# A two-block sequence model on one core: the second block's input scaled once, its products read from PSUM, and all low parts of the recurrent mixer on VectorE

## The chip, the cores and the metric

The kernel runs on one core of a Trainium2 chip, as one launch. The metric is the time of the whole program on the device, in microseconds (us). TensorE is the matrix engine (PE in the profile), VectorE is DVE, ScalarE is ACT, GpSimd is POOL, and SyncE (SP) issues most of the DMA transfers.

## The reference

Two residual blocks over 256 tokens with 2048 features, all in float32. The first block (a state-space mixer beside latent attention, and a feed-forward part) is not touched by the change. The second block computes, cut to what matters:

```
u = rms_norm(h, norm1_g);  P = u @ w_in_2
z, xbc, dt_raw = parts of P                      # state-space mixer
pr = rest of P;  pr = pr + (prev_token(pr) - pr) * mu   # recurrent mixer
xbc = silu(causal_conv4(xbc));  xs, B, C = xbc
y_ssd = group_norm(scan(xs, dt, A, B, C) + D * xs, times silu(z)) * g
r, k, v, wd, ad, gd = pr                         # three of 2048, and low-rank inputs
y_rwkv = per head: S = S*decay + (S a) b^T + v k^T;  y = S r, then norm, bonus, gate
h = h + concat(y_ssd, y_rwkv) @ w_out_2
h = h + (silu(v @ w_gate) * (v @ w_up)) @ w_down,  v = rms_norm(h, norm2_g)
out = rms_norm(h, norm_f_g)
```

The input h of the second block is the first block's final norm of its own sum. Both norms are one factor per token and a gain per feature, so that P = R(token) * ((gains * sum) @ w_in_2).

## The kernel before

Features lie on the 128 partitions and the 256 tokens along the free dimension, so a matrix product makes an output tile of 128 features by 256 tokens in one PSUM bank. Each f32 operand is split into a rounded high part and a low part (the difference), and a product is the sum of high x low, high x high and low x high. `split` makes the two parts of an input tile (ScalarE the high, VectorE the low one). `piece` loads 512 KB of weights (`raw`), ScalarE rounds them (`wh`, L329) and VectorE or GpSimd subtracts (`wl`, L335): `self.pl` is the share of pieces whose subtraction goes to GpSimd. It is 0 in the state-space stage, 1 in the recurrent stage and on into the output product, and 0.25 in the feed-forward part. `gemm` runs 2 pieces and 16 x 3 matmuls of 256 columns in these stages (`self.one`), and after each 16th part calls `tick`, which steps the background work of the recurrent mixer.

The stages of the second block, with their times in the profile: `block2_pre` (norm factors, from 1206 us), `ssd_phase` (4 products for low-rank inputs and step sizes with `ssd_dt`, 8 for B and C, 16 pairs for x and z; to about 1506), `rwkv_phase` (16 times k, v and r, then the first half of the output product with the state-space result; to about 2190), `block2_out` (second half of the output product) and `ffn2`.

Here the products are made on the unscaled input tiles (`xx`), and the norm's factor R is multiplied into every product when it leaves PSUM: `shift_mix` and `conv_silu` call `evac` (L381, VectorE, PSUM times R into a tile `ev`), then a ScalarE step and one or three VectorE steps (L1113, the token shift; L1128, the convolution's taps) read `ev`. `ssd_pair` does the same for z with Rh = R / 2 (tile `zh`). Two PSUM banks (`acc`) take turns for the products.

In the recurrent stage the order of TensorE's instructions is the program's, written by hand with `tick` counts (`TK`); the other engines' orders, and all of the state-space stage, come from a scheduler that simulates the engines. Heads are worked in 8 groups of two tiles. For each group there are masked products (L1446 to L1464), an inverse of a triangular block by a loop of 30 small VectorE steps (L1494, L1496) with round trips through DRAM, and then 4 recurrence steps: TensorE, the copy `ws` (L1569), TensorE, the copies into `UV` (L1574), TensorE, the new state (L1583).

Of the kernel before, what the change touches and what calls it, by code (L numbers as in the profile page):

```python
# [10 lines left out]
F32 = mybir.dt.float32  # L11
# [7 lines left out]
P = 128  # L19
T = 256  # L20
# [203 lines left out]
class K:  # L224
# [851 lines left out]
    def block2_pre(self, p1):  # L1076
# [14 lines left out]
        self.bcast(r2, self.R)  # L1091
        nc.gpsimd.tensor_scalar(self.Rh, self.R, 0.5, None, ALU.mult)
        self.bcast(r1, self.R1)
# [12 lines left out]

    def shift_mix(self, p, out, i):

        nc = self.nc
        a = self.t(tag="ev")  # L1110
        self.evac(p, a, self.R, eng=nc.gpsimd)
        nc.scalar.activation(out, a, AF.Copy, scale=self.omm[:, i:i + 1])
        nc.vector.scalar_tensor_tensor(out[:, 1:], a[:, :T - 1], self.v("mu", i), out[:, 1:], ALU.mult, ALU.add)  # L1113

    def conv_silu(self, p, out, i):

        nc = self.nc
        a = self.t(tag="ev")
        self.evac(p, a, self.R, eng=nc.gpsimd)
# [57 lines left out]
    def ssd_group(self, g, pb, pc):  # L1177

        nc = self.nc
        B = self.t(tag="sB", bufs=2)  # L1180
        self.conv_silu(pb, B, 16 + g)
        C = self.CC[:, g]
        self.conv_silu(pc, C, 20 + g)
        p = self.ps(384, "pcs")
        nc.tensor.transpose(p[:, :P], B[:, :P], self.ident)
        for b in range(2):
            sl = slice(b * P, b * P + P)
            nc.tensor.matmul(p[:, P + b * P:2 * P + b * P], B[:, sl], C[:, sl], start=True, stop=True)
        nc.scalar.activation(self.BT[:, g], p[:, :P], AF.Copy)
        nc.vector.tensor_tensor(self.CC[:, 4 + g].rearrange("p (c t) -> p c t", c=2),  # L1190
                                p[:, P:].rearrange("p (c t) -> p c t", c=2),
                                self.tri.unsqueeze(1).to_broadcast([P, 2, P]), op=ALU.mult)

    def ssd_pair(self, j, px, pz):
# [67 lines left out]
    def ssd_phase(self, xx):  # L1262
        nc, A = self.nc, self.A
        W = A["w_in2"]
        self.tri = self.sd.tile([P, P], F32, name="tri")
        nc.scalar.dma_start(self.tri, A["cst3"])
        self.CC = self.b([8, T], "hh0")
        self.BT = self.b([4, P], "hh1")
        p = self.gemm(W[0], 16, xx)
        x0 = self.t(tag="ev")  # L1270
        self.shift_mix(p, x0, 48)
        self.twd = self.m2.tile([P, T], F32, name="twd")
        nc.scalar.activation(self.twd, x0, AF.Tanh)
        self.ssd_dt(x0)
        self.tad = self.m2.tile([P, T], F32, name="tad")
        self.shift_mix(self.gemm(W[1], 16, xx), self.tad, 49)
        self.tgd = self.m2.tile([P, 2, T], F32, name="tgd")
        for i in range(2):
            x0 = self.t(tag="ev")
            self.shift_mix(self.gemm(W[2 + i], 16, xx), x0, 50 + i)  # L1280
            nc.scalar.activation(x0, x0, AF.Tanh, scale=0.5)
            nc.vector.tensor_scalar(self.tgd[:, i], x0, 1.0, 0.5, ALU.add, ALU.mult)
        for g in range(4):
            pb = self.gemm(W[4 + g], 16, xx)
            pc = self.gemm(W[8 + g], 16, xx)
            self.ssd_group(g, pb, pc)
        for j in range(16):
            px = self.gemm(W[12 + j], 16, xx)
            pz = self.gemm(W[28 + j], 16, xx)
            for _ in self.ssd_pair(j, px, pz):  # L1290
                pass


    def rwkv_alloc(self):
        nc, c = self.nc, self.rw
        xb = self.b([16, T], "X")
        bk = xb[:, 0:8].rearrange("p (s c) t -> p s (c t)", s=4).rearrange("p s (c t) -> p s c t", c=4)
        nc.gpsimd.memset(bk, 0.0)
# [4 lines left out]

        self.BK = xb[:, 8:16].rearrange("p (i h) t -> p i h t", i=4).rearrange("p i h (c n) -> p i h c n", c=4)
# [4 lines left out]
        self.Gs = self.b([4, 2, 4, 64], "B0")  # L1309
        self.UV = self.b([4, 2, 4, 64], "B1")  # L1310
        nc.gpsimd.memset(self.L, 0.0)
# [305 lines left out]
    def rwkv_phase(self, xx):  # L1617
        nc, V = self.nc, self.nc.vector
        W = self.A["w_in2"]
        self.rwkv_alloc()  # L1620
        self.pl = 1
        self.rs_ = {}
        with self.tc.manual_schedule(engines={mybir.EngineType.PE}):
# [16 lines left out]

            xs = self.xx_new()
            for k in range(16):
# [32 lines left out]
    def block2(self, xx, p1, upto=99):  # L1675
# [3 lines left out]
        with ExitStack() as es0:  # L1679
            self.m2 = es0.enter_context(self.tc.tile_pool(name="m2", bufs=1))  # L1680
            with ExitStack() as es:
# [3 lines left out]
                self.sd = self.ph = es.enter_context(self.tc.tile_pool(name="sd", bufs=1))  # L1685
                self.ssd_phase(xx)
            if upto < 4:
# [24 lines left out]
    def block2_out(self):  # L1712
        nc, A = self.nc, self.A
        V = nc.vector
        x0 = self.b([8, 2, T], "X", F32R)
        x1 = [self.b([4, 2, T], f"xx{i}", F32R) for i in range(2)]

        def xs(k):
            return x0[:, k] if k < 8 else x1[k // 4 - 2][:, k % 4]

        for k in range(16):
# [3 lines left out]
        for i in range(2):  # L1725
            nc.sync.dma_start(self.hh[i], self.hd2[:, 8 * i:8 * i + 8])
        self.x2 = [self.b([4, 2, T], t, F32R) for t in ("B0", "B1", "xx2", "xx3")]
        pf = Sums(self, 16)
        for n in range(16):
            p = self.gemm(A["w_out2"][16 + n], 16, xs)  # L1730
            self.add_h(p, n)
            self.split(self.x2[n // 4][:, n % 4], self.h(n), self.v("norm2_g", n))
            pf.add(self.h(n))
        self.pf = pf.out

    def ffn2(self):
# [5 lines left out]

        def x2(k):
            return self.x2[k // 4][:, k % 4]

        for half in range(2):
            a0 = self.b([8, 2, T], "X", F32R)
            a1 = [self.b([4, 2, T], f"xx{i}", F32R) for i in range(2)]
            a2 = self.f.tile([P, 6, 2, T], F32R, name=self.nm("ac"), tag="ac")

            def ac(k, a0=a0, a1=a1, a2=a2):
                return a0[:, k] if k < 8 else a1[k // 4 - 2][:, k % 4] if k < 16 else a2[:, k - 16]

# [72 lines left out]
```

## Time and profile before

| what | value |
|---|---|
| median of 3 runs | 3052.31 us (3050.88 to 3054.97) |
| the profiled execution's own time | 3044.86 us |
| its span, first to last instruction | 3043.1 us |
| TensorE busy, share of the span | 2826.2 us, 93% |
| VectorE busy | 2004.5 us, 66% |
| ScalarE busy | 1521.5 us, 50% |
| GpSimd busy | 1267.5 us, 42% |
| mean granted TensorE clock | 0.965 |
| low parts on VectorE, on GpSimd | 522 of 1280 ns mean, 351 of 2396 ns mean |

Busy time is the time in which an engine has an instruction under way; matmuls overlap in a pipeline, so a busy TensorE need not be at its peak. The granted clock is a share of 2.4 GHz. A wait is put down to the instruction that ended last before the waiting one began.

### The profile page before, as it was taken

The numbers are of one execution on the slowest core, as the hardware profiler recorded it, in microseconds if no ns is written. First come the engines' busy times: TensorE is split into PE (matmuls) and PEld (weight loads), VectorE is DVE, ScalarE is ACT, GpSimd is POOL, SyncE is SP. The second block draws the span as 40 slices with busy tenths as digits, with TensorE's granted clock in tenths as the row PEclk, the third lists the DMA queues.
The fourth block names the chain that finished last, engine by engine and source line by source line (L and its number), as shares of the span: only waits on it lengthen the run. The fifth ranks groups of instructions, "written<-read, shape, count | busy, mean of one in ns | idle before, by whom it ended". The sixth has DMA issues, their size and how long they took to land.

```text
span 3043.1 us, 54949 instructions
## 1 busy us (share of the span) xinstructions
PE 2826.2 (93%) x21648; PEld 2543.3 (84%) x21648; DVE 2004.5 (66%) x3272; ACT 1521.5 (50%) x2553; POOL 1267.5 (42%) x877
## 2 busy tenths in 40 slices
PE   6766999999999999999979888888899999999998
PEld 6755988888888888999878878778888888888887
DVE  9994578885388866887676777775365554355544
ACT  6527555554455555555445444453354444444454
POOL 6555663333333344011465444444694333233333
PEclk8878999999999999999999999999999999999999
DMA  4222355556655566555443333334655556655565
GB/s 164 84 78 70 110 169 184 186 187 182 189 185 186 189 179 222 186 180 182 149 131 111 109 106 107 108 112 155 215 181 187 189 187 187 192 191 186 189 186 154
DMA packets 178979, 490.38 MB, mean 161 GB/s; under 512 B 44416, under 2 KB 61600, under 8 KB 178208
## 3 DMA queue, kind: packets, MB, share of 16 engines
q1 hardware_dynamic: 176992, 483.13, 50.1%
q8 instruction: 170, 2.79, 0.4%
q0 software_dynamic: 288, 2.10, 0.2%
q10 hardware_dynamic: 1440, 1.63, 0.2%
q14 instruction: 89, 0.73, 0.1%
HBM read 474.17 MB, written 12.62 MB: 160 GB/s over the span
## 4 chain that ended last, share of the span: by engine, by line
PE 69%; DVE 8%; DMA 3%; issue 1%; POOL 1%; ACT 1%; SPq 1%; POOLq 0%; DVEq 0%; ACTq 0%
PE acc L353 34%; PE acc L354 17%; PE acc L349 5%; PE acc L350 4%; PE acc L351 4%; DVE ti L1494 1%; DVE D L1496 1%; POOL wl L335 1%; DVE kvr L1113 1%; ACT wh L329 1%; PE pm L1446 1%; DMA N<-n_d 1%; PE pc L1329 1%; DMA raw<-in_w_in_dram 0%; DVE kvr L1457 0%
## 5 line engine op out<-in xcount | busy, mean ns | idle before, releaser
L329 ACT ACTIVATE wh<-raw 128x1024 fp32r<-128x1024 f32 (+2 forms) x873 | 907.8, 1041 | 948.0 <-PE acc L353 459.2
L335 POOL TENSOR_TENSOR wl<-raw,wh 128x1024 fp32r<-128x1024 f32 (+1 forms) x351 | 839.6, 2396 | 815.0 <-ACT wh L329 785.0
L335 DVE TENSOR_TENSOR wl<-raw,wh 128x1024 fp32r<-128x1024 f32 (+2 forms) x522 | 667.8, 1280 | 481.7 <-ACT wh L329 478.2
L353 PE MATMUL acc<-xx,wh 128*128 128x512 f32 x2496 | 885.8, 395 | 0.0
L354 PE MATMUL acc<-xx,wl 128*128 128x256 f32 x2496 | 704.3, 282 | 0.0
L349 PE MATMUL acc<-xx,wh 128*128 128x256 f32 x1968 | 599.7, 305 | 19.6 <-ACT wh L329 7.4
L351 PE MATMUL acc<-xx,wl 128*128 128x256 f32 x1968 | 567.8, 289 | 15.1 <-POOL wl L335 11.0
L350 PE MATMUL acc<-xx,wh 128*128 128x256 f32 x1968 | 568.0, 289 | 0.0
L353 PEld LDWEIGHTS acc<-xx,wh 128*128 128x128 f32 x2496 | 469.9, 188 | 110.6
L354 PEld LDWEIGHTS acc<-xx,wl 128*128 128x128 f32 x2496 | 468.9, 188 | 4.5 <-POOL wl L335 3.9
L349 PEld LDWEIGHTS acc<-xx,wh 128*128 128x128 f32 x1968 | 386.0, 196 | 33.4 <-ACT wh L329 8.1
L351 PEld LDWEIGHTS acc<-xx,wl 128*128 128x128 f32 x1968 | 385.8, 196 | 18.2 <-POOL wl L335 12.5
L350 PEld LDWEIGHTS acc<-xx,wh 128*128 128x128 f32 x1968 | 387.0, 197 | 2.8 <-issue 1.2
L353 PE MATMUL acc<-B,wh 128*128 128x512 f32 x960 | 341.1, 394 | 0.0
L354 PE MATMUL acc<-B,wl 128*128 128x256 f32 x960 | 269.6, 281 | 2.0 <-DVE wl L335 1.0
L353 PE MATMUL acc<-X,wh 128*128 128x512 f32 x640 | 230.5, 397 | 2.2 <-ACT wh L329 2.2
L390 POOL TENSOR_TENSOR ev<-ev,R 128x256 f32<-128x256 f32 x88 | 70.7, 803 | 353.5 <-PE acc L353 322.2
L353 PEld LDWEIGHTS acc<-B,wh 128*128 128x128 f32 x960 | 180.6, 188 | 41.7
L213 POOL TENSOR_TENSOR qa<-qa,sq 128x256 f32<-128x256 f32 x86 | 88.4, 1028 | 281.7 <-issue 133.7
L354 PEld LDWEIGHTS acc<-B,wl 128*128 128x128 f32 x960 | 179.8, 187 | 3.1 <-POOL wl L335 1.6
L354 PE MATMUL acc<-X,wl 128*128 128x256 f32 x640 | 180.8, 282 | 1.6 <-POOL wl L335 1.6
L353 PEld LDWEIGHTS acc<-X,wh 128*128 128x128 f32 x640 | 121.4, 190 | 29.5 <-ACT wh L329 2.4
(491 smaller groups left out, 4228.9 us busy)
## 6 DMA issues: line engine op xcount, KB each, us to landing
raw<-in_w_up_dram SPq DMA_DIRECT2D x264, 512.0 KB, 3.7
raw<-in_w_in_dram SPq DMA_DIRECT2D x213, 512.0 KB, 3.7
raw<-in_w_down_dram SPq DMA_DIRECT2D x128, 448.0 KB, 3.8
raw<-in_w_out_dram SPq DMA_DIRECT2D x96, 512.0 KB, 3.7
raw<-in_w_gate_dram SPq DMA_DIRECT2D x88, 512.0 KB, 4.2
raw<-in_w_down_dram SPq DMA_DIRECT2D x64, 512.0 KB, 4.2
raw<-in_w_glu_dram SPq DMA_DIRECT2D x8, 512.0 KB, 3.4
cb<-cs_d SPq DMA_DIRECT2D x16, 256.0 KB, 4.1
```

What stands on the lines that cost most here:

```text
L213: nc.gpsimd.tensor_tensor(self.acc, self.acc, sq, op=ALU.add)
L329: nc.scalar.activation(h, r, AF.Copy)
L335: eng.tensor_tensor(l, r, h.bitcast(F32), op=ALU.subtract)
L349: nc.tensor.matmul(p[:, :T], h, x[:, 1], start=first, stop=False)
L350: nc.tensor.matmul(p[:, :T], h, x[:, 0], start=False, stop=False)
L351: nc.tensor.matmul(p[:, :T], l, x[:, 0], start=False, stop=last)
L353: nc.tensor.matmul(p, h, x.rearrange("p a b -> p (a b)"), start=first, stop=False)
L354: nc.tensor.matmul(p[:, T:], l, x[:, 0], start=False, stop=last)
L390: (eng or nc.vector).tensor_tensor(out, s, mul, op=ALU.mult)
L1113: nc.vector.scalar_tensor_tensor(out[:, 1:], a[:, :T - 1], self.v("mu", i), out[:, 1:], ALU.mult, ALU.add)
L1329: self.nc.tensor.matmul(out[hs], lhsT[hs], rhs[hs], start=start, stop=stop)
L1446: nc.tensor.matmul(p[:, P * c:P * c + P], z[:, c], AR[:, c].rearrange("p a t -> p (a t)"), start=True, stop=True)
```

## The change

After the first use of the input, each of the 16 input tiles is made anew from the sum h, with the gains and R multiplied in, and split (`rescale`, four tiles behind each of the first four products, into buffers X, B0, B1). The 4 first products and the 8 for B and C still use the unscaled tiles and `evac`; the 32 of the pairs and the 48 of the recurrent mixer use the scaled ones, and what follows reads PSUM directly (`rms` returns the bank). The factor 1/2 of z goes into the tanh's scale and the last product of a pair, so Rh is not made there. `self.pl = 1` is taken out of the recurrent stage: the share stays 0 until `ffn2` sets 0.25, so all low parts there and in the output product are VectorE's. The buffers of the recurrent mixer move from X, B0, B1 to xx0 to xx3, and those of the output product and the feed-forward part change to fit.

```diff
-        nc.gpsimd.tensor_scalar(self.Rh, self.R, 0.5, None, ALU.mult)
+        self.cg = self.m2.tile([P, 16], F32, name="cg2")
+        nc.vector.tensor_tensor(self.cg, self.vs("final_norm_w"), self.vs("norm1_g"), op=ALU.mult)
...
+    def x16(self):
+        a, b, c = self.b([8, 2, T], "X", F32R), self.b([4, 2, T], "B0", F32R), self.b([4, 2, T], "B1", F32R)
+        return lambda k: a[:, k] if k < 8 else b[:, k - 8] if k < 12 else c[:, k - 12]
+    def rescale(self, xs, ks):
+        for k in ks:
+            t = self.t(tag="ev")
+            self.nc.vector.scalar_tensor_tensor(t, self.h(k), self.cg[:, k:k + 1], self.R, ALU.mult, ALU.mult)
+            self.split(xs(k), t)
+    def rms(self, p, scaled):
+        if scaled:
+            return p[:, :T]
         a = self.t(tag="ev")
-        self.evac(p, a, self.R, eng=nc.gpsimd)
+        self.evac(p, a, self.R)
+        return a
+    def shift_mix(self, p, out, i, scaled=True):
+        a = self.rms(p, scaled)
...
-        self.evac(pz, zh, self.Rh, eng=nc.gpsimd)
-        nc.scalar.activation(th, zh, AF.Tanh)
-        V.scalar_tensor_tensor(zh, th, 1.0, zh, ALU.add, ALU.mult)
+        nc.scalar.activation(th, pz[:, :T], AF.Tanh, scale=0.5)
+        V.scalar_tensor_tensor(zh, th, 1.0, pz[:, :T], ALU.add, ALU.mult)
...
-        V.tensor_tensor(y, x, zh, op=ALU.mult)
+        V.scalar_tensor_tensor(y, x, 0.5, zh, ALU.mult, ALU.mult)
...
-        self.CC = self.b([8, T], "hh0")
-        self.BT = self.b([4, P], "hh1")
         p = self.gemm(W[0], 16, xx)
         x0 = self.t(tag="ev")
-        self.shift_mix(p, x0, 48)
+        xs = self.x16()
+        self.shift_mix(p, x0, 48, False)
+        self.rescale(xs, range(4))
...
-            px = self.gemm(W[12 + j], 16, xx)
-            pz = self.gemm(W[28 + j], 16, xx)
+            px = self.gemm(W[12 + j], 16, xs)
+            pz = self.gemm(W[28 + j], 16, xs)
...
-        self.pl = 1
```

## Rows read from the trace of the kernel before

**Rows 1.** Busy time by stage: us, PE, PEld, DVE, ACT, POOL, PEclk, DMA share, GB/s.
```profile
1213.00:1290.00 77.00, 76.56 (x639) 76.56 (x640) 67.89 (x137) 40.95 (x65) 0.50 (x1) 0.98 0.58 189
1290.00:1490.00 200.00, 200.00 (x1679) 190.39 (x1678) 160.16 (x320) 102.95 (x177) 25.12 (x24) 1.00 0.56 178
1490.00:1506.00 16.00, 10.43 (x84) 9.02 (x82) 9.06 (x12) 4.87 (x8) 11.05 (x7) 0.85 0.43 142
1506.00:2190.00 684.00, 599.44 (x6977) 553.27 (x6978) 447.69 (x934) 304.44 (x589) 343.57 (x195) 0.95 0.40 123
2190.00:2300.00 110.00, 105.14 (x583) 88.47 (x583) 62.80 (x60) 56.05 (x91) 92.72 (x47) 0.97 0.62 203
```

**Rows 2.** Waits, 1506 to 2190: us in total, times, longest us.
```profile
POOL wl L335 <- ACT wh L329: 255.0, 88, 10.4
...
PE pc L1329 <- DVE ws L1569: 36.0, 12, 5.0
```

**Rows 3.** Timeline of TensorE: start, us, instruction, [idle before <- releaser].
```profile
1759.12 1.16 PE L1446 MATMUL pm<-hh,X 128*128 128x128 f32 x8 [2.62 <-DVE yc L1614]
...
1796.06 0.69 PE L1329 MATMUL pc<-ws,hh 64*64 64x64 f32 x8 [3.53 <-DVE ws L1569]
```

**Rows 4.** TensorE alone in one stretch: us, PE, PEclk, DMA share, GB/s.
```profile
1796.00:1800.00 4.00, 3.94 (x19) 0.50 0.07 27
```

**Rows 5.** Timeline of VectorE.
```profile
1751.14 0.42 DVE L1439 TENSOR_TENSOR hh<-kvr,rv 128x256 f32<-128x256 f32 x1
...
1756.26 2.47 DVE L1457 SCALAR_TENSOR_TENSOR kvr<-kvr,vec,kvr 128x256 f32<-128x256 f32 x1
...
1778.64 0.19 DVE L1494 TENSOR_TENSOR ti<-D,N 128x30 f32<-128x30 f32 x1
...
1790.74 2.50 DVE L1439 TENSOR_TENSOR hh<-kvr,rv 128x256 f32<-128x256 f32 x1
...
1797.36 0.48 DVE L1457 SCALAR_TENSOR_TENSOR kvr<-kvr,vec,kvr 128x256 f32<-128x256 f32 x1
```

**Rows 6.** Timeline of GpSimd.
```profile
1755.91 2.54 POOL L335 TENSOR_TENSOR wl<-raw,wh 128x1024 fp32r<-128x1024 f32 x1 [5.48 <-ACT wh L329]
...
1788.03 4.93 POOL L335 TENSOR_TENSOR wl<-raw,wh 128x1024 fp32r<-128x1024 f32 x2 [1.63 <-ACT wh L329]
```

**Rows 7.** VectorE by line, 1506 to 2190: busy us, mean ns, idle before.
```profile
L1113 DVE SCALAR_TENSOR_TENSOR kvr<-ev,vec,kvr 128x255 f32<-128x255 f32 x48 | 77.4, 1612 | 52.6 <-ACT kvr L1112 52.6
L1494 DVE TENSOR_TENSOR ti<-D,N 128x30 f32<-128x30 f32 (+10 forms) x120 | 49.0, 409 | 14.7 <-DMA N<-n_d 11.6
L1496 DVE TENSOR_TENSOR D<-D,ti 128x30 f32<-128x30 f32 (+10 forms) x120 | 40.8, 340 | 3.3
...
L1413 DVE TENSOR_TENSOR X<-kvr,rv 64x256 f32<-64x256 f32 x32 | 21.9, 684 | 0.6
L381 DVE TENSOR_TENSOR ev<-acc,R 128x256 f32<-128x256 f32 x47 | 19.9, 423 | 41.0 <-PE acc L351 40.7
...
L1648 DVE SCALAR_TENSOR_TENSOR ev<-ev,vec,R 128x256 f32<-128x256 f32 x16 | 18.2, 1135 | 20.4 <-DMA ev<-h_d 19.9 <-DVE ev L1649 0.6
L1457 DVE SCALAR_TENSOR_TENSOR kvr<-kvr,vec,kvr 128x256 f32<-128x256 f32 x16 | 17.7, 1106 | 0.2
L1439 DVE TENSOR_TENSOR hh<-kvr,rv 128x256 f32<-128x256 f32 x13 | 15.9, 1223 | 0.1
...
L1403 DVE SCALAR_TENSOR_TENSOR rv<-kvr,vec,pn 128x256 f32<-128x256 f32 x16 | 7.6, 476 | 2.3 <-PE pn L1365 2.1
```

**Rows 8.** GpSimd by line, 1506 to 2190.
```profile
L335 POOL TENSOR_TENSOR wl<-raw,wh 128x1024 fp32r<-128x1024 f32 x123 | 294.6, 2399 | 269.0 <-ACT wh L329 255.0 <-DMA lw<-in_lora_dram 7.2 <-DMA raw<-in_w_in_dram 5.1
L1359 POOL TENSOR_TENSOR hoe<-hne,mhalf 128x4 f32<-128x4 f32 x16 | 16.6, 1036 | 24.0 <-DVE hne L1356 15.7 <-DVE hnl L1358 8.3
```

**Rows 9.** VectorE by line, state-space stage, 1213 to 1490.
```profile
L335 DVE TENSOR_TENSOR wl<-raw,wh 128x1024 fp32r<-128x1024 f32 x81 | 99.2, 1225 | 16.4 <-ACT wh L329 15.5
```

**Rows 10.** Timeline of VectorE at the end of the state-space stage.
```profile
1499.78 2.39 DVE L1248 TENSOR_TENSOR yg<-sx,zh 128x256 f32<-128x256 f32 x1
```

More of the change, by code (lines that the diff above doesn't have):

```diff
@@ L1105, in block2_pre, with conv_silu @@
         nc.vector.tensor_scalar(self.oka, self.vs("k_a"), -0.5, 1.0, ALU.mult, ALU.add)
-    def shift_mix(self, p, out, i):
+    def x16(self):
[9 more added lines that the diff above has]
+            return p[:, :T]
+        a = self.t(tag="ev")
+        self.evac(p, a, self.R)
+        return a
+    def shift_mix(self, p, out, i, scaled=True):
         nc = self.nc
-        a = self.t(tag="ev")
-        self.evac(p, a, self.R, eng=nc.gpsimd)
+        a = self.rms(p, scaled)
         nc.scalar.activation(out, a, AF.Copy, scale=self.omm[:, i:i + 1])
         nc.vector.scalar_tensor_tensor(out[:, 1:], a[:, :T - 1], self.v("mu", i), out[:, 1:], ALU.mult, ALU.add)
-    def conv_silu(self, p, out, i):
+    def conv_silu(self, p, out, i, scaled=True):
         nc = self.nc
-        a = self.t(tag="ev")
-        self.evac(p, a, self.R, eng=nc.gpsimd)
+        a = self.rms(p, scaled)
         y = self.t(tag="ev")
@@ L1180, in ssd_group @@
         B = self.t(tag="sB", bufs=2)
-        self.conv_silu(pb, B, 16 + g)
+        self.conv_silu(pb, B, 16 + g, False)
         C = self.CC[:, g]
-        self.conv_silu(pc, C, 20 + g)
+        self.conv_silu(pc, C, 20 + g, False)
         p = self.ps(384, "pcs")
@@ L1275, in ssd_phase @@
         self.tad = self.m2.tile([P, T], F32, name="tad")
-        self.shift_mix(self.gemm(W[1], 16, xx), self.tad, 49)
+        self.shift_mix(self.gemm(W[1], 16, xx), self.tad, 49, False)
+        self.rescale(xs, range(4, 8))
         self.tgd = self.m2.tile([P, 2, T], F32, name="tgd")
@@ L1279, in ssd_phase @@
             x0 = self.t(tag="ev")
-            self.shift_mix(self.gemm(W[2 + i], 16, xx), x0, 50 + i)
+            self.shift_mix(self.gemm(W[2 + i], 16, xx), x0, 50 + i, False)
+            self.rescale(xs, range(8 + 4 * i, 12 + 4 * i))
             nc.scalar.activation(x0, x0, AF.Tanh, scale=0.5)
             nc.vector.tensor_scalar(self.tgd[:, i], x0, 1.0, 0.5, ALU.add, ALU.mult)
+        self.CC = self.b([8, T], "hh0")
+        self.BT = self.b([4, P], "hh1")
         for g in range(4):
@@ L1287, in ssd_phase @@
         for j in range(16):
-            px = self.gemm(W[12 + j], 16, xx)
-            pz = self.gemm(W[28 + j], 16, xx)
+            px = self.gemm(W[12 + j], 16, xs)
+            pz = self.gemm(W[28 + j], 16, xs)
             for _ in self.ssd_pair(j, px, pz):
                 pass
+        return xs
     def rwkv_alloc(self):
         nc, c = self.nc, self.rw
-        xb = self.b([16, T], "X")
-        bk = xb[:, 0:8].rearrange("p (s c) t -> p s (c t)", s=4).rearrange("p s (c t) -> p s c t", c=4)
+        bk = self.b([8, T], "xx0").rearrange("p (s c) t -> p s (c t)", s=4).rearrange("p s (c t) -> p s c t", c=4)
         nc.gpsimd.memset(bk, 0.0)
@@ L1302, in sets @@
             return x.rearrange("p i (c t) -> p i c t", c=4)
-        self.BK = xb[:, 8:16].rearrange("p (i h) t -> p i h t", i=4).rearrange("p i h (c n) -> p i h c n", c=4)
+        self.BK = self.b([8, T], "xx1").rearrange("p (i h) t -> p i h t", i=4).rearrange("p i h (c n) -> p i h c n", c=4)
         x = self.b([4, 4, 2, 64], "hh0")
@@ L1308, in rwkv_alloc @@
         self.Nc, self.L = sets(x[:, 0:4]), sets(x[:, 4:8])
-        self.Gs = self.b([4, 2, 4, 64], "B0")
-        self.UV = self.b([4, 2, 4, 64], "B1")
+        self.Gs = self.b([4, 2, 4, 64], "xx2")
+        self.UV = self.b([4, 2, 4, 64], "xx3")
         nc.gpsimd.memset(self.L, 0.0)
@@ L1639, in rwkv_phase @@
                 self.spawn(self.rwkv_r(st, self.gemm(W[44 + j], 16, xx)))
-            xs = self.xx_new()
+            xs = self.x16()
             for k in range(16):
@@ L1685, in block2 @@
                 self.sd = self.ph = es.enter_context(self.tc.tile_pool(name="sd", bufs=1))
-                self.ssd_phase(xx)
+                xx = self.ssd_phase(xx)
             if upto < 4:
@@ L1714, in block2_out @@
         V = nc.vector
[L1715 to L1719, printed above, removed]
+        xs = self.xx_new()
         for k in range(16):
@@ L1726, in block2_out @@
             nc.sync.dma_start(self.hh[i], self.hd2[:, 8 * i:8 * i + 8])
-        self.x2 = [self.b([4, 2, T], t, F32R) for t in ("B0", "B1", "xx2", "xx3")]
+        self.x2 = self.x16()
         pf = Sums(self, 16)
@@ L1731, in block2_out @@
             self.add_h(p, n)
-            self.split(self.x2[n // 4][:, n % 4], self.h(n), self.v("norm2_g", n))
+            self.split(self.x2(n), self.h(n), self.v("norm2_g", n))
             pf.add(self.h(n))
@@ L1741, in ffn2, with ac @@
         self.pl = 0.25
-        def x2(k):
-            return self.x2[k // 4][:, k % 4]
+        x2 = self.x2
         for half in range(2):
-            a0 = self.b([8, 2, T], "X", F32R)
-            a1 = [self.b([4, 2, T], f"xx{i}", F32R) for i in range(2)]
+            a1 = self.xx_new()
             a2 = self.f.tile([P, 6, 2, T], F32R, name=self.nm("ac"), tag="ac")
-            def ac(k, a0=a0, a1=a1, a2=a2):
-                return a0[:, k] if k < 8 else a1[k // 4 - 2][:, k % 4] if k < 16 else a2[:, k - 16]
+            def ac(k, a1=a1, a2=a2):
+                return a1(k) if k < 16 else a2[:, k - 16]
             for i in range(22):
```

## The prediction

> **What bounds the kernel now.** I read first the busy time by stage [rows 1]. TensorE is near full everywhere except in one long stage: in the state-space stage (1213 to 1490 us) it shows no idle worth naming, while in the recurrent stage (1506 to 2190 us) it is busy for 599.44 of 684 us, so 84.6 us are idle, at a mean granted clock of 0.95. Every instruction that TensorE issues there is issued after the change too, so what can be won is its idle time and its slow time. The slow time, by the same row: (1 - 0.95) x 599 = 30 us. Together 115 us, the most that this stage can give. No step of the change touches the stages before 1206 us or the second feed-forward part but by its buffers.
>
> Next, who TensorE waits for. The chain of waits says VectorE: the recurrence's copy `ws` (L1569) alone ends 12 waits, 36.0 us, longest 5.0 [rows 2]. Two such waits are shown with their length [rows 3]: 2.62 us before 1759.12 and 3.53 us before 1796.06. The granted clock of the 4 us behind the second is 0.50 [rows 4], the lower level of the two (1.2 GHz) after that idle: a wait costs its length and then again in slow matmuls.
>
> Then what VectorE does in front of these [rows 5]. At 1756.26 an operation of 128x256 elements (L1457) takes 2.47 us, at 1790.74 another (L1439) 2.50 us; the same two lines take 0.42 (at 1751.14) and 0.48 (at 1797.36) elsewhere. Beside them GpSimd makes a low part, `wl`, from 1755.91 for 2.54 us and two from 1788.03 for 4.93 us [rows 6]: the VectorE operation ends when GpSimd's does. So VectorE, when it reads both operands from SBUF, stands still while GpSimd reads SBUF in a `wl`. The operations that read one operand from PSUM are not stretched: L1403 has a mean of 476 ns, L381 of 423 [rows 7]. The list by line gives the price of it in the stage, mean against unstretched time: L1113 77.4 - 48 x 0.48 = 54.4 us; L1494 and L1496 89.8 - 240 x 0.19 (the row at 1778.64) = 44.2; L1439 15.9 - 13 x 0.42 = 10.4; L1648 18.2 - 16 x 0.48 = 10.5; L1457 17.7 - 16 x 0.48 = 10.0; L1413 21.9 - 32 x 0.42 = 8.5. Sum 138 us [rows 5, 7], in stretches of about 1.9 us (2.4 - 0.45), so some 73 blocked operations for 123 `wl` on GpSimd [rows 8].
>
> **The change part by part.**
>
> *Low parts from GpSimd to VectorE, recurrent stage.* 123 pieces leave GpSimd at 2.40 us [rows 8] and come to VectorE at 1.225 us, its mean in the state-space stage [rows 9]: +151 us. Gone are the 138 us of blocking, and the 47 products with R from PSUM, 19.9 us [rows 7]. VectorE's busy time goes from 447.7 to 447.7 + 151 - 138 - 20 = 441 us: no lighter, but made of shorter pieces. What TensorE feels is how long an urgent small operation (`ws`, `UV`, the masked products) waits in VectorE's queue, and that goes with the sum of squared durations of what may stand in front. Before: 73 x 2.4^2 = 420, and some 310 us of short work at about 0.4 us, 310 x 0.4 = 124; together 544. After: 123 x 1.225^2 = 185, and 290 x 0.4 = 116; 301, a ratio of 0.55. I take the 115 us of idle and slow time down in that ratio: -52 us. Both ends: if none of the waits hang on this, 0; if all end, -115. I take the middle value, since in both waits looked at the blocked operation's excess (2.0 and 2.1 us) is most of the wait, yet a `wl` of 1.2 us ready at the same moment may stand in its place.
>
> *Products read from PSUM.* In the recurrent stage ScalarE and then VectorE (L1113) read the bank itself. L1113 is then a PSUM reader at 0.48 us, and its value comes one queue entry of 0.42 us sooner. The bank is held longer, until L1113 ends; `acc` has two, and the bank is wanted again only after another product of 48 matmuls, so I cost that at nothing. The cover is the other bank's product: if L1113 ends later than that, TensorE stands for the difference. In the state-space stage 32 products with R or Rh go (0.42 us each as L381 in [rows 7], so 13.4 us), three taps and one ScalarE step read the bank, and TensorE there has no idle to give back: 0.
>
> A rule of the Trainium skill speaks against this part: "VectorE: DVE Perf Modes", Rules for kernel authors, says that elementwise work on a matmul's output should copy PSUM to SBUF first if many operations follow, since a PSUM source runs at the lowest rate. By it the taps would lengthen; the rows of L1403 (476 ns, one PSUM operand) and of L1457 unstretched (480 ns, SBUF alone) [rows 5, 7] show no difference in f32, so by the rows the sum stays as it is, and by the rule it would lose some of the 13.4 us, hidden behind a full TensorE.
>
> *Input scaled once.* 16 tiles, each a product on VectorE (0.48 us), a copy on ScalarE and a difference on VectorE (0.42): 14.4 us of VectorE work, put among the first four products, just where VectorE is fullest: 67.89 of 77 us from 1213 to 1290 [rows 1]. 67.9 + 14.4 = 82.3, over 77 by 5 us. The rescaled tiles are wanted only by the thirteenth product and the chain for the step sizes (`ssd_dt`) has its result wanted by the first pair, so what could be late is a `wl`, and three buffers of it stand between. From 1290 on VectorE has 40 us free in 200 and 13.4 us fewer to do, and takes the backlog. Bounds: 0 (the slack takes all) to +8 (5 us of backlog in front of `wl`, and a clock that falls behind it); I take +3. Buffers `hh0` and `hh1` now wait for the last rescaling before the first group writes them; that is inside the same +3. No DMA is added or moved, and Rh's product on GpSimd (one) goes with no reader left.
>
> *End of the state-space stage.* From 1490 to 1506 TensorE is busy for 10.43 of 16 us [rows 1]; L1248 there, 128x256 elements from SBUF, takes 2.39 us in place of some 0.45, blocked by a `wl` of the recurrent stage's first products [rows 10]. Bounds 0 and -5.6; I take -3.
>
> *Output product.* GpSimd's share stays in force into the output product in the kernel before (GpSimd busy 92.72 of 110 us from 2190 on [rows 1]). Its 32 pieces come to VectorE: 32 x 1.225 = 39 us beside 62.8, less its own blocking, in 110: it fits under TensorE's 105.14. If it didn't, the 5 us of TensorE idle there would grow by the overshoot. Renamed buffers come free before the rows that fill them: 0.
>
> Sum: -52 + 3 - 3 = -52 us. The profiled execution took 3044.86 us for a span of 3043.1; it lies 7.5 us under the median of 3052.31. By its own time the result is 2993, as a median 3052.3 - 52 = 3000.
>
> By the Trainium skill, "SBUF — State Buffer", Who interferes with whom, a VectorE instruction with two SBUF inputs stands for the whole of a GpSimd instruction that reads SBUF. By that the 16 power operations of L1359 (1.04 us each [rows 8]), which stay on GpSimd, would go on blocking, at most 16.6 us of VectorE time. For the long `wl` the rows agree with it; the sum above leaves the 16.6 us out of before and after alike.
>
> **The rivals.**
>
> 1. *All waits end* (-90 to -121, that is 115 and 5.6: 2931 to 2962). For it: both waits looked at follow a blocked operation directly. Against: VectorE stays 441 us busy in some 630.
> 2. *The waits move.* Queueing is as long as before because a `wl` is ready at the moments at which the operation was blocked: 1.2 us in place of 1.9, and TensorE's order, written by ticks, keeps the rest. At 0 to 0.6 us for each of the 32 steps of the recurrence (8 groups of 4) the gain is 0 to 19 us: 3033 to 3052. For it: VectorE's total does not fall.
> 3. *Slower: VectorE waits in order for ScalarE.* GpSimd's idle time in front of `wl` is 255 us, waiting for the high part [rows 8], harmless on GpSimd. On VectorE everything behind such a `wl` waits too. It is 88 waits [rows 2], 2.9 us each; if each of the 32 steps has one in front, 32 x 2.9 = 93 us against the 52 gained: 3052 + 41 = 3093. It decides from 52 / 32 = 1.6 us per step. Against: in the state-space stage VectorE makes all `wl` and waits 15.5 us for 81 of them [rows 9], 0.19 us each.
>
> **How the numbers follow.** Forecast (gain of 20 to 90 us) 0.64; rival 1 0.10; rival 2 0.14, of which 0.06 within 0.2% (about 6 us, what a measurement of this kernel can tell from no change) and 0.08 faster by more; slower 0.12, of it 0.10 for rival 3 and 0.02 for a backlog at the start that outlasts its bound. Faster 0.64 + 0.10 + 0.08 = 0.82, same 0.06, slower 0.12. The likeliest is 3000. The range runs from 2940 (about half of rival 1's chance left out) to 3055 (rival 3 left out, and little else), some 0.16 outside.
>
> **What the profile would show.** Right: L1113 near 0.48 us in every instance; no VectorE operation of 2 us but the reciprocal; VectorE's total in the stage near 440 us; the stage shorter by about 50 us, TensorE's idle in it near 45 us, clock near 0.97; the state-space stage as long as before within 5 us. Wrong: VectorE rows idle before `wl`, released by ScalarE, for more than 60 us; TensorE waiting for `wl` at the start of the state-space stage, or for an `acc` bank; blocked operations gone and the waits for `ws` as long as before.

## The result, and the profile after

The changed kernel takes 2956.88 us (median of 4 runs, 2956.44 to 2960.41) against 3051.6 (4 runs, 3049.77 to 3054.97) for the kernel before, run beside it: a ratio of 0.9691, 95% interval 0.9674 to 0.9708, which is 95 us less. The forecast was 3000; the time lies in the band of rival 1 (2931 to 2962).

The profiled execution has a span of 2954.8 us and a mean clock of 0.973. The busy time by stage of the changed kernel, with the columns of [rows 1] (us, PE, PEld, DVE, ACT, POOL, PEclk, DMA share, GB/s):

```profile
1213.00:1290.00 77.00, 76.12 (x632) 75.95 (x633) 73.27 (x154) 42.86 (x73) 1.81 (x1) 0.98 0.52 173
1290.00:1490.00 200.00, 197.92 (x1667) 187.98 (x1666) 149.75 (x302) 104.20 (x183) 19.28 (x22) 1.00 0.58 185
1490.00:1506.00 16.00, 12.10 (x105) 11.03 (x104) 10.55 (x22) 5.64 (x10) 3.45 (x4) 0.92 0.52 176
1506.00:2103.00 597.00, 575.47 (x6992) 535.35 (x6991) 416.05 (x1012) 306.12 (x596) 56.34 (x72) 0.98 0.47 142
2103.00:2213.00 110.00, 109.05 (x634) 95.01 (x635) 77.44 (x93) 59.25 (x93) 21.90 (x19) 1.00 0.63 206
```

The recurrent stage takes 597 us in place of 684 [rows 1]. That is 87 of the 88.3 us between the two spans; the median fell by 7 us more, as the profiled execution of before lay that far under its median. TensorE's idle time in the stage went from 84.6 to 21.5 us, its slow time from 30 to (1 - 0.98) x 575 = 11.5: together from 115 to 33.

VectorE by line in that stage (busy us, mean ns, idle before), the lines of [rows 7] among it. Line numbers stand some 20 higher than before: L1113 is now L1133, L1494 and L1496 are L1516 and L1518, L1413 is L1435, L1457 is L1479, L1439 is L1461.

```profile
L335 DVE TENSOR_TENSOR wl<-raw,wh 128x1024 fp32r<-128x1024 f32 x123 | 150.8, 1226 | 81.3 <-ACT wh L329 79.6
...
L1133 DVE SCALAR_TENSOR_TENSOR kvr<-acc,vec,kvr 128x255 f32<-128x255 f32 x48 | 23.0, 478 | 12.2 <-ACT kvr L1132 11.7
L1518 DVE TENSOR_TENSOR D<-D,ti 128x30 f32<-128x30 f32 (+10 forms) x120 | 22.0, 183 | 3.1
L1516 DVE TENSOR_TENSOR ti<-D,N 128x30 f32<-128x30 f32 (+10 forms) x120 | 21.9, 182 | 9.9 <-DMA N<-n_d 7.1
...
L1435 DVE TENSOR_TENSOR xx<-kvr,rv 64x256 f32<-64x256 f32 x32 | 13.4, 417 | 0.5
...
L1479 DVE SCALAR_TENSOR_TENSOR kvr<-kvr,vec,kvr 128x256 f32<-128x256 f32 x16 | 7.8, 485 | 0.2
...
L1461 DVE TENSOR_TENSOR hh<-kvr,rv 128x256 f32<-128x256 f32 x13 | 5.5, 419 | 0.0
```

Every line is back at its unstretched time: L1133 at 478 ns where it had 1612, L1516 at 182 where it had 409. If one counts each VectorE operation of the stage that lies over 0.8 us above the shortest of its line and shape, and adds up what it lies above, the stage before has 80 such operations with 154 us, the stage after none. These are the "blocked" operations in what follows.

The waits of the stage (us in total, times, longest):

```profile
DVE wl L335 <- ACT wh L329: 79.6, 44, 4.8
...
PE pz L1549 <- DVE zt L1540: 10.6, 4, 4.9
...
PE pc L1351 <- DVE ws L1591: 1.0, 1, 1.0
```

TensorE's waits for the recurrence's copy `ws` fell from 36.0 us to 1.0 [rows 2]. VectorE now waits for ScalarE's high part, as rival 3 said that it would, for 79.6 us, and TensorE does not feel it. On the page, the chain of work that ended last has become TensorE's: 78% of the span (69% before), and VectorE's share of it 2% (8% before).

### The profile page after: what moved, and what is told of

Read it like the earlier page. It is cut to its first block, busy times and chain, and to the rows that moved or that the text cites. A ratio compares the mean times of both kernels' runs of the same rounds, so it can differ in the third digit from the quotient of the medians.

```text
span 2954.8 us, 54809 instructions
## 1 busy us (share of the span) xinstructions
PE 2808.0 (95%) x21648; PEld 2530.9 (86%) x21648; DVE 1974.3 (67%) x3385; ACT 1523.8 (52%) x2569; POOL 889.5 (30%) x716
## 4 chain that ended last, share of the span: by engine, by line
PE 78%; DMA 2%; DVE 2%; ACT 1%; SPq 1%; issue 1%; POOL 0%; POOLq 0%; DVEq 0%; ACTq 0%
PE acc L353 35%; PE acc L354 18%; PE acc L349 7%; PE acc L350 6%; PE acc L351 6%; PE pc L1351 1%; PE pm L1468 1%; DVE wl L335 1%; PE pm L1630 1%; PE pc L1356 1%; PE py L1259 0%; DMA n_d<-hh 0%; PE pm L1351 0%; SPq L1532 0%; ACT wh L329 0%
## 5 line engine op out<-in xcount | busy, mean ns | idle before, releaser
L335 DVE TENSOR_TENSOR wl<-raw,wh 128x1024 fp32r<-128x1024 f32 (+2 forms) x682 | 861.1, 1263 | 602.7 <-ACT wh L329 595.8
L354 PE MATMUL acc<-xx,wl 128*128 128x256 f32 x2176 | 614.7, 283 | 0.8 <-DVE wl L335 0.8
L335 POOL TENSOR_TENSOR wl<-raw,wh 128x1024 fp32r<-128x1024 f32 (+1 forms) x191 | 454.6, 2381 | 532.4 <-ACT wh L329 517.0
L353 PEld LDWEIGHTS acc<-xx,wh 128*128 128x128 f32 x2176 | 409.9, 188 | 99.1 <-ACT wh L329 0.7
L354 PEld LDWEIGHTS acc<-xx,wl 128*128 128x128 f32 x2176 | 409.7, 188 | 1.5 <-DVE wl L335 1.4
L349 PE MATMUL acc<-B,wh 128*128 128x256 f32 x960 | 287.5, 300 | 5.6 <-ACT xx L379 3.2
L350 PE MATMUL acc<-B,wh 128*128 128x256 f32 x960 | 272.5, 284 | 0.0
L351 PE MATMUL acc<-B,wl 128*128 128x256 f32 x960 | 272.2, 284 | 0.0
L354 PE MATMUL acc<-B,wl 128*128 128x256 f32 x960 | 271.2, 282 | 1.0 <-POOL wl L335 1.0
L354 PE MATMUL acc<-X,wl 128*128 128x256 f32 x960 | 270.8, 282 | 0.0
L349 PE MATMUL acc<-X,wh 128*128 128x256 f32 x832 | 251.2, 302 | 5.8 <-ACT wh L329 4.5
L351 PE MATMUL acc<-X,wl 128*128 128x256 f32 x832 | 235.5, 283 | 0.8 <-DVE wl L335 0.8
L350 PE MATMUL acc<-X,wh 128*128 128x256 f32 x832 | 235.1, 283 | 0.0
L353 PEld LDWEIGHTS acc<-B,wh 128*128 128x128 f32 x960 | 180.5, 188 | 43.4
L349 PEld LDWEIGHTS acc<-B,wh 128*128 128x128 f32 x960 | 184.2, 192 | 11.3 <-ACT xx L379 3.4
L350 PEld LDWEIGHTS acc<-B,wh 128*128 128x128 f32 x960 | 184.3, 192 | 0.6
```

The lines of the kernel that those rows point to most:

```text
L335: eng.tensor_tensor(l, r, h.bitcast(F32), op=ALU.subtract)
L349: nc.tensor.matmul(p[:, :T], h, x[:, 1], start=first, stop=False)
L350: nc.tensor.matmul(p[:, :T], h, x[:, 0], start=False, stop=False)
L351: nc.tensor.matmul(p[:, :T], l, x[:, 0], start=False, stop=last)
L353: nc.tensor.matmul(p, h, x.rearrange("p a b -> p (a b)"), start=first, stop=False)
L354: nc.tensor.matmul(p[:, T:], l, x[:, 0], start=False, stop=last)
```

## Experiments

The theories. A: VectorE stood still while GpSimd read SBUF, and the end of this is the gain. Against it: the gain comes from the other half of the change, products that are read from PSUM at once and 47 VectorE steps fewer; or it comes from the low part itself, which took GpSimd 2.40 us and takes VectorE 1.23, so that it was ready later. The expectations name theories by letters and say in words what each would give. No experiment leaves out any part of the computation; some add work whose result nobody reads. The kernel before was run beside them each time, and the ratios are to it: 3052.85 us for experiments 1 to 4, 3061.95 for 5, 6, 8 and 9, and 3056.58 for 7 and 10 to 12.

**1. The low parts alone.** The kernel before, with one line gone:

```diff
-        self.pl = 1
```

> The kernel before with one line taken out: GpSimd's share of the low parts in the recurrent stage and the output product is 0; the norm's factor is still multiplied in when a product leaves PSUM. Theory A (VectorE stands still while GpSimd reads SBUF for a low part, and the gain is the end of that): no blocked VectorE operation is left, and most of the 95 us gained comes back, 65 to 90 us, so 2962 to 2987 us; L1113 near 0.48 us though both its operands lie in SBUF. Rival B (the gain comes from the products read from PSUM, one queue entry less per product): at most 25 us gained, 3027 to 3052. Rival C (VectorE has no room for 123 low parts beside the 48 products with R): slower than 3052.

Measured: 2955.89 us, ratio 0.969 (0.9671 to 0.9708): the whole gain. No blocked operation is left in the stage, and TensorE's waits for `ws` fall to 0.2 us. The operations of one line of this kernel, by the tile that they write (min/median/max ns, first and last start):

```profile
L1113 DVE SCALAR_TENSOR_TENSOR kvr<-ev,vec,kvr x48: 473/477/484, 1507.3 to 1965.2; 128x255 f32<-128x255 f32 x48
```

The same code, SBUF operands and all, took 2294 ns in the median before. Scaling the input and reading PSUM add nothing to it: 2956.88 with them, 2955.89 without.

**2. The PSUM reads alone.** The changed kernel, with the share put back:

```diff
+        self.pl = 1
```

> The changed kernel with GpSimd's share put back to 1 in the recurrent stage and the output product; input scaled once, products read from PSUM. Theory A: some 100 blocked operations less those that now read PSUM (48 of L1133 are safe), so the blocked time falls from about 153 us to 90 to 120, and 20 to 45 us are gained: 3007 to 3032 us. Rival B: nearly the whole gain stays, 2957 to 2985. If both parts were needed together: 3045 to 3060.

Measured: 3018.74 us, ratio 0.9893 (0.9874 to 0.9912): 34 us gained. 68 blocked operations with 113 us are left. The same view:

```profile
L1133 DVE SCALAR_TENSOR_TENSOR kvr<-acc,vec,kvr x48: 441/482/485, 1513.6 to 2016.6; 128x255 f32<-128x255 f32 x48
L1435 DVE TENSOR_TENSOR xx<-kvr,rv x32: 409/422/2578, 1531.0 to 2029.3; 64x256 f32<-64x256 f32 x32
```

GpSimd works as before here, yet none of the 48 operations of L1133 is stretched, since one operand now comes from PSUM; L1435, with both from SBUF, still reaches 2578 ns. So the two parts of the change cure the same thing: the PSUM reads take one line out of GpSimd's way, and where GpSimd is gone there is nothing left for them to do. How much of the 34 us is instead the 47 VectorE steps fewer (19.9 us of its time [rows 7]) no run shows.

**3 and 4. GpSimd reads, GpSimd writes.** All low parts stay VectorE's, and GpSimd gets an operation of its own on the low part's buffer, ahead of VectorE's. It reads SBUF in one kernel (1.61 us in the mean) and only writes it in the other (three fills of 0.66 us in the mean):

```diff
 (in piece, recurrent stage only: experiment 3)
+            nc.gpsimd.tensor_tensor(l[:, :800], self.vec[:, :800], self.vec[:, :800], op=ALU.subtract)
 (experiment 4)
+            for w in (800, 800, 400):
+                nc.gpsimd.memset(l[:, :w].bitcast(F32), 0.0)
```

> The changed kernel, with one more GpSimd instruction for each low part of the recurrent stage: it subtracts a constant from itself (800 elements from SBUF, some 1.9 us) into the tile of the low part, before VectorE writes the real one over it. It adds nothing to VectorE. Theory A: VectorE operations with two SBUF operands are again blocked, 40 to 90 of them, and the stage grows by 25 to 80 us: 2982 to 3037 us. Rival D (the gain came from low parts that are ready sooner): the longer way to a low part costs as much here as in the run with writes only; the difference of the two is under 6 us.

> As the run in which GpSimd reads, but GpSimd only writes constants into the same tile (three fills, 800, 800 and 400 elements, about the same time in all), so it is as much in the way of the low part, and reads no SBUF. Theory A: no blocked VectorE operation; 2957 to 2975 us, at least 20 us less than the run in which GpSimd reads. Rival D: both runs lose the same, and more than 20 us.

Measured: 3025.58 us with the reads (ratio 0.9917, 0.9895 to 0.9938) and 2970.08 with the writes (0.9735, 0.9715 to 0.9755). VectorE by line with the reads:

```profile
L1521 DVE TENSOR_TENSOR D<-D,ti 128x30 f32<-128x30 f32 (+10 forms) x120 | 41.4, 345 | 3.2
...
L1438 DVE TENSOR_TENSOR xx<-kvr,rv 64x256 f32<-64x256 f32 x32 | 24.1, 752 | 0.3
```

and with the writes:

```profile
L1522 DVE TENSOR_TENSOR D<-D,ti 128x30 f32<-128x30 f32 (+10 forms) x120 | 22.6, 188 | 3.3
...
L1439 DVE TENSOR_TENSOR xx<-kvr,rv 64x256 f32<-64x256 f32 x32 | 13.3, 416 | 0.2
```

One blocking, seen in the timeline of the kernel with the reads:

```profile
1710.95 1.88 POOL L337 TENSOR_TENSOR wl<-vec 128x800 fp32r<-128x800 f32 x1 [2.78 <-PE acc L354]
...
1711.36 1.51 DVE L1521 TENSOR_TENSOR D<-D,ti 128x33 f32<-128x33 f32 x1
```

VectorE's operation begins 0.41 us into GpSimd's and ends with it, at 1712.87 and 1712.83; its own work is 0.18 us. With the writes the buffer goes through GpSimd just as it does with the reads, and the low part is delayed no less: VectorE waits 41.1 us for GpSimd ahead of its low parts there, 32.8 us with the reads. That delay costs 13 us over the changed kernel. The further 55 us are the reading. So the third theory holds for a small part at most, and A for the rest.

**5. Half of the low parts.** The changed kernel, with `self.pl = 0.5` in the recurrent stage (in force through the output product, as in experiment 2):

> The changed kernel with GpSimd's share of the low parts at one half in the recurrent stage and the output product (it is 0 there; with 1 it took 3018.7 us, with 0 2956.9). If the loss goes with the number of low parts on GpSimd: half of 62 us, 2975 to 3000 us, some 25 to 40 blocked operations. If VectorE's relief pays for the blocking at a middle share: 2950 or less. If one blocked operation for each step of the recurrence is enough for the whole loss: above 3005.

Measured: 2961.79 us, ratio 0.9682 (0.9654 to 0.9711), not to be told from the changed kernel's 0.9691. 17 operations of the stage are blocked, with 31 us, and the stage is as long as without them:

```profile
1506.00:2103.00 597.00, 574.62 (x6990) 533.84 (x6988) 376.62 (x948) 303.48 (x595) 203.65 (x133) 0.98 0.46 141
```

A cost in proportion to the blocking would have been 17 / 68 of the 62 us by which experiment 2 lies above the changed kernel, some 16 us. So none of the expected cases came: what is lost does not grow evenly with the blocked time. Two things can be the reason, and this run does not part them: TensorE may have some slack against VectorE, so that blocking costs only what goes beyond it, or VectorE's relief (377 us of work in the stage in place of 416) may pay for the blocking.

**6 and 7. VectorE with more to do.** To see whether there is slack and where it ends, VectorE is loaded without any blocking. Once the 800-element subtraction of experiment 3 is put on VectorE, ahead of the low part; then, since there it can wait for the buffer, a second subtraction of 800 elements is put behind the low part, where all its operands are there:

```diff
 (experiment 6, ahead of the low part)
+            nc.vector.tensor_tensor(l[:, :800], self.vec[:, :800], self.vec[:, :800], op=ALU.subtract)
 (experiment 7, behind it)
+            nc.vector.tensor_tensor(l[:, :800], r[:, :800], h[:, :800].bitcast(F32), op=ALU.subtract)
```

> The changed kernel, with one more VectorE instruction for each low part of the recurrent stage: the same subtraction of 800 elements that GpSimd did in the run in which it reads, now on VectorE (about 0.95 us each, some 117 us in all). VectorE gets about the work that the blocking took from it, but in the order that the scheduler planned with. Theory E (the stretch hurts because it is not in the plan and falls on the operation that is due): little is lost, 2957 to 2975 us. Theory F (any longer work in VectorE's queue costs TensorE by its squared length, as the prediction's sum had it: 123 x 0.95^2 = 111 of 544, of 115 us): 23 us more, 2975 to 2990. If VectorE simply runs out of room: above 3010.

> The changed kernel, with 800 of the 1024 elements of each low part of the recurrent stage subtracted a second time by VectorE, behind the first time (some 0.97 us each, 119 us in all). Unlike the run with an extra VectorE instruction ahead of the low part (3077 us), this one waits for no buffer of its own: the buffer is its already. Theory E (VectorE has room for planned work; there the loss was the wait for the buffer at the head of VectorE's queue): 2957 to 2985 us, and VectorE's idle time ahead of its low parts, released by TensorE, is near 0. Theory F (VectorE is out of room, whatever the order): again above 3040.

Measured: 3077.37 us (ratio 1.0057, 1.0037 to 1.0077) and 3086.99 (1.0094, 1.0076 to 1.0112): both slower than the kernel before by under 1%, with no operation blocked. Experiment 6 went past what theories E and F gave it, into its third case (above 3010), and experiment 7 came out as theory F had it. In experiment 6 VectorE waits 78.6 us at the head of its queue for the buffer; experiment 7 has no such wait, and is no faster, so the wait isn't needed for the loss. The added work by line, TensorE's wait for it at one group, and the stage, all of experiment 7 (the last with the columns of the stages above):

```profile
L338 DVE TENSOR_TENSOR wl<-raw,wh 128x800 fp32r<-128x800 f32 x123 | 121.9, 992 | 1.2
```

```profile
1744.98 1.07 PE L1552 MATMUL pz<-zt,hh 32*32 32x32 f32 x64 [14.19 <-DVE zt L1543]
```

```profile
1506.00:2234.00 728.00, 592.11 (x6998) 549.37 (x6998) 525.02 (x1137) 311.37 (x598) 58.74 (x73) 0.90 0.39 118
```

VectorE was idle for 597 - 416 = 181 us of the stage; 122 us of added work lengthen it by 131. The place is the loop of 30 small steps (L1516 and L1518 in the changed kernel), each of which needs the one before. From its first to its last step it takes 13.0 us in the changed kernel (mean of the 8 groups) and 26.7 here. A part of it near its beginning, in VectorE's timeline of experiment 7:

```profile
1708.79 0.17 DVE L1521 TENSOR_TENSOR D<-D,ti 128x15 f32<-128x15 f32 x1
1708.90 1.23 DVE L336 TENSOR_TENSOR wl<-raw,wh 128x1024 fp32r<-128x1024 f32 x1
1710.04 0.17 DVE L1519 TENSOR_TENSOR ti<-D,N 128x14 f32<-128x14 f32 x1
1710.24 0.48 DVE L1608 SCALAR_TENSOR_TENSOR sv<-pc,PC,sv 128x64 f32<-128x64 f32 x2
1710.63 0.98 DVE L338 TENSOR_TENSOR wl<-raw,wh 128x800 fp32r<-128x800 f32 x1
1711.53 0.17 DVE L1521 TENSOR_TENSOR D<-D,ti 128x14 f32<-128x14 f32 x1
```

A low part stands between the first step shown and the second, which needs it, and the repeat of one between the second and the third. The loops grew by 8 x 13.7 = 110 us. TensorE's waits for `zt`, the loop's result, grew by about as much, to 118.8 us in 8 waits from 10.6 in 4 in the changed kernel. This is not the place where the blocking had cost most: in the kernel before the loop took 13.6 us in the mean, and TensorE waited 8.3 us for `zt` in the whole stage.

**8 and 9. The same in the first block.** The first block's mixers give GpSimd shares of 0 to 1 by stage, in a list. The changed kernel, with the shares gone in all of it, or only from the fourth entry on:

```diff
-PB = [0.0, 0.625, 1.0, 1.0, 0.625, 0.625]
+PB = [0.0, 0.0, 0.0, 0.0, 0.0, 0.0]
 (the other)
+PB = [0.0, 0.625, 1.0, 0.0, 0.0, 0.0]
```

> The changed kernel, with GpSimd's share of the low parts set to 0 in the first block's mixers as well (it is 0.625 to 1 there). If the trade of the recurrent stage holds there: blocked operations there (some 113 us of VectorE time up to 470 us) end, 10 to 40 us faster, 2917 to 2947. If VectorE is the bound of that stage (it is busy for 77.58 of 80 us from 150 to 230): slower, 2960 to 2985, as each low part there comes on top of a full engine.

> The changed kernel, with GpSimd's share set to 0 only from the attention part of the first block on (from about 230 us; VectorE is busy for about 60% there), and left as it is in the scan before. If blocking costs TensorE there too: 3 to 20 us faster, 2937 to 2954. If those waits hang on other engines: 2953 to 2961.

Measured: 2906.42 us (ratio 0.9501, 0.9478 to 0.9525) and 2933.64 (0.9591, 0.9566 to 0.9616), both faster than the ranges expected. Two VectorE lines of the first block in the changed kernel:

```profile
L620 DVE TENSOR_TENSOR B<-ef,ef 64x256 f32<-64x256 f32 x32 | 23.4, 732 | 4.2 <-PE sp L659 3.8
...
L1004 DVE TENSOR_TENSOR hh<-hh,ev 128x256 f32<-128x256 f32 x16 | 18.9, 1183 | 0.6
```

and with all shares gone:

```profile
L620 DVE TENSOR_TENSOR B<-ef,ef 64x256 f32<-64x256 f32 x32 | 15.6, 487 | 1.0 <-PE sp L659 0.6
...
L1004 DVE TENSOR_TENSOR hh<-hh,ev 128x256 f32<-128x256 f32 x16 | 6.9, 430 | 0.6
```

Up to 470 us, 46 blocked operations with 86 us become 5 with 9. With a bound of 0.3 us in place of 0.8, the excess goes from 121 us to 49; GpSimd keeps other work in this block, and where those shorter stretches come from was not looked into. The first load of the block's feed-forward weights goes from 431.0 us to 391.7, 39 of the 50 us gained. This is the fastest kernel here, 156 us under the kernel before as it ran beside it.

**10 to 12. Around that kernel.** The kernel before with the shares gone in both blocks' mixers and nothing else; experiment 8 with the feed-forward parts' shares of 0.25 gone as well; experiment 8 with a share of 0.25 in the recurrent stage:

```diff
 (10, on the kernel before)
+PB = [0.0, 0.0, 0.0, 0.0, 0.0, 0.0]
-        self.pl = 1
 (11, on experiment 8, in both feed-forward parts)
-        self.pl = 0.25
+        self.pl = 0
 (12, on experiment 8, in the recurrent stage)
+        self.pl = 0.25
```

> The kernel before with nothing changed but GpSimd's shares: 0 in the first block's mixers and 0 in the recurrent stage and the output product; products still multiplied by R when they leave PSUM. If the scaled input and the reads from PSUM give nothing once GpSimd makes no low parts there (as the run with the low parts alone says): the same as the changed kernel with the first block's shares at 0, 2906 us, within 6: 2900 to 2912.

> The changed kernel with the first block's shares at 0 and the feed-forward parts' shares (0.25) at 0 too, so that VectorE makes every low part of the kernel. TensorE has no idle time to give back in the feed-forward parts (659 of 660 us busy in the first): 2900 to 2910 us, the same as 2906. If VectorE's extra pieces get late there: 2912 or more.

> The changed kernel with the first block's shares at 0, and a quarter of the low parts of the recurrent stage and output product on GpSimd. Half a share cost 5 us there in place of the 31 that a loss in proportion would be. If a few blocked operations are absorbed: 2903 to 2909, the same as 2906. If VectorE's relief is worth something: 2890 to 2903. If every blocked operation costs its part of the 62 us: 2915 to 2925.

Measured: 2914.37 us (0.9529, 0.9507 to 0.955), 2910.06 (0.9516, 0.9498 to 0.9534) and 2919.2 (0.9547, 0.9529 to 0.9565). The first two are not to be told from experiment 8, so scaling the input and reading PSUM are worth nothing that shows in the faster kernel either, and the feed-forward shares are indifferent. Experiment 10 lies 2 us above its expected range. The quarter share costs some 13 us against experiment 8, with intervals that just part, and 5 and 9 us against experiments 10 and 11, which ran beside it; by its time that is the last of its expected cases. The half share had cost 5 us or nothing in experiment 5. The traces show one difference: from 1456 to 2063 us, which is this stage there, the quarter share blocks 16 operations with 31 us, about as much as the half share does, though half as many pieces are GpSimd's (31 in place of 62). VectorE is relieved of 8 us by it and of 39 by the half share, and the stage ends 10 us later than in experiment 8. That speaks for the relief as what paid in experiment 5; it is not shown.

## Why the prediction was right and wrong

**Bound and place: right.** TensorE's idle and slow time in the recurrent stage was the 115 us to be won, and 87 of the 88.3 us came out of that stage.

**Mechanism: right.** The chain from a `wl` on GpSimd through a stretched VectorE operation to a late result was read from two waits [rows 3, 5, 6]; the first of them was released by `yc` (L1614), and only the second by `ws`. Experiments 1, 3 and 4 show each link: the waits for `ws` go from 36.0 us to 0.2 without the low parts on GpSimd, and 12.2 us come back with its reads. By the Trainium skill, "SBUF — State Buffer", Who interferes with whom, an operation with two SBUF inputs is not blocked by a GpSimd instruction that only writes; experiment 4 agrees (188 ns where reads made it 345).

**The failed step: the size of -52.** The step is the ratio 301 / 544 = 0.55 of squared durations, applied to the 115 us. The measured ratio is 33 / 115 = 0.29, and the term is -82 (-87 by the stage's length). Its inputs were nearly right: 123 low parts at 1.226 us, as costed at 1.225, and 154 us of blocking where six lines gave 138. (The 310 us of short work hold some 33 us of the blocked operations a second time; without them the ratio is 0.57.) The form was wrong, and to both sides. By it the 123 pieces of 0.99 us that experiment 7 adds would cost 121 / 544 of 115 us, some 26 us; they cost 131. It let TensorE feel every piece in front of an urgent operation alike, whatever slack that operation had. What stands in its place is shown only in part. Experiment 7 shows one edge: 122 us more, none of it longer than a low part, and 108 us of TensorE's waiting appear in the dependent loop, where little was lost before the change. Experiment 5 has 17 blocked operations at no cost that shows, but experiment 12 has 16 that come with a stage 10 us longer, so it is no proof of slack. That the changed kernel stands just short of that edge is a reading, not shown. The -52 was the middle between 0 and -115; what spoke for the far end, that the excess was most of both waits looked at, was the better guide.

**VectorE's total: 416 us, forecast 441.** Some 16 of the 25 us are the blocking that the six lines did not hold.

**Products from PSUM: 0 beside the moved low parts, as costed; 34 us alone.** The bank's longer hold was costed at nothing, and cost one wait. In the state-space stage a product's first matmul waits for the last of the convolution's taps (L1147), which now reads the bank; a low part and two other steps of VectorE's stand between the taps. A wait for an `acc` bank was one of the signs of being wrong:

```profile
1301.85 0.39 PE L349 MATMUL acc<-X,wh 128*128 128x256 f32 x1 [1.32 <-DVE ev L1147]
```

The rule of the Trainium skill ("VectorE: DVE Perf Modes", Rules for kernel authors) leaves two ways open, to accept the rate of a PSUM source or to copy to SBUF first where many operations follow. Here no difference shows between the sources: 478 ns from PSUM (L1133 after), 477 from SBUF (experiment 1).

**Input scaled once: costed at +3, and at most half of that.** TensorE's idle time from 1213 to 1490 us went from 0.44 to 0.88 + 2.08 = 2.96 us, of which 1.32 are the wait above. Another of the waits, in TensorE's timeline of the changed kernel:

```profile
1238.29 0.36 PE L349 MATMUL acc<-xx,wh 128*128 128x256 f32 x1 [0.76 <-DVE ev L381]
```

**End of the state-space stage: costed at -3.** Idle 5.57 to 3.90 us, slow time 1.6 to 1.0: -2.3.

**Output product: costed at 0.** In its second half TensorE is busy for 109.05 of 110 us at a clock of 1.00, so the 32 pieces fit. The renamed buffers were costed at 0 as well, but the first matmul of its first half now waits for ScalarE's high part, as it does neither in the kernel before nor in experiment 1, which keeps the old buffers:

```profile
1963.61 0.39 PE L349 MATMUL acc<-X,wh 128*128 128x256 f32 x1 [4.53 <-ACT wh L329]
```

**Readings that were off.** Of the unstretched times in [rows 5], 0.42 us is L1439's and 0.48 is L1457's, which the prediction's sentence turns round; its sum has them right. Both stretched operations end 0.28 us after GpSimd's low part. And that a wait is paid again in slow matmuls was read behind one of the two waits: behind the other, from 1759 to 1763 us, the granted clock was 1.00.

**Rivals.** The first came out, all waits end; against it I had set that VectorE stays busy for 441 of 630 us, and a busy share of 70% in 597 turned out to leave enough room. The second did not come. The third's wait came, 79.6 us in 44 waits, above the 60 us that I had named as a sign of being wrong: a wait of an engine says nothing as long as what is queued behind it isn't due. In experiment 7 it is just as long (80.2 us in 30 waits), and the loss there is the loop's.

**Open.** Whether half the low parts on GpSimd cost so little because TensorE has slack or because VectorE is relieved, and why a quarter of them blocks as much as a half. A half share on top of experiment 8 wasn't tried.

## What to carry to other kernels

Before half of an elementwise job goes to GpSimd, look in the timeline for VectorE operations that end when a GpSimd operation ends: 123 pieces moved off VectorE (151 us of its time) cost it 154 us of standing still, and the kernel 95. Do not sum such pieces to predict what a bound engine feels; find the chain of dependent small operations, its slack, and whether the pieces in front of it exceed that. And try each half of a change alone: here one deleted line was all of it, and the same deletion in another block was worth 50 us more.

## What the runs showed of the hardware

- A VectorE operation with one operand in PSUM is not held up by GpSimd's reads: 482 ns in the median and 485 at most of 48, beside GpSimd's 2.4 us low parts (experiment 2), where the form with SBUF operands had a median of 2294. In all, 165 VectorE operations that read PSUM begin inside one of these low parts, and none is more than 0.05 us over its shortest.
- Two operands in SBUF are not needed for being held up. L1408, which reads one tile of 128x256 elements and writes the same one, takes 0.28 us alone; in experiment 2 it falls beside the low parts, and 13 of 16 are stretched by over 0.5 us:

```profile
L1408 DVE TENSOR_SCALAR rv<-rv x16: 278/1303/1822, 1514.0 to 1994.4; 128x256 f32<-128x256 f32 x16
```

- GpSimd's writes hold up no VectorE operation with two SBUF operands: 218 of them begin inside one of the memsets of 800, 800 and 400 elements before each low part, and none is more than 0.04 us over its shortest (experiment 4); the subtractions that read 800 elements left 51 blocked operations (experiment 3). The one blocked operation of experiment 4 is that same form with one SBUF operand (L1412 there), 1.20 us beside memsets in place of 0.28.
- Not every GpSimd operation that reads SBUF holds VectorE up for its length. The power operations stay on GpSimd (16 of 4 elements a partition and 8 of 8), and the timeline of the changed kernel shows one with the loop's steps, both operands in SBUF, at their usual length inside it. In the whole stage 30 VectorE operations with two SBUF operands begin inside one of the 24, and none is more than 0.05 us over its shortest:

```profile
1740.97 1.01 POOL L1381 TENSOR_TENSOR hoe<-hne,mhalf 128x4 f32<-128x4 f32 x1 [6.92 <-DVE hne L1378]
...
1741.40 0.18 DVE L1516 TENSOR_TENSOR ti<-D,N 128x30 f32<-128x30 f32 x1
1741.61 0.19 DVE L1518 TENSOR_TENSOR D<-D,ti 128x30 f32<-128x30 f32 x1
1741.84 0.19 DVE L1516 TENSOR_TENSOR ti<-D,N 128x30 f32<-128x30 f32 x1
```

The prediction weighed the Trainium skill's rule ("SBUF — State Buffer", Who interferes with whom) that the block lasts for the whole of GpSimd's instruction. For the low parts it does; for these operations of 4 elements a partition the row decides against it, and the up to 16.6 us that the rule would have added do not exist.
